# A fused two-layer transformer block on one core: operand rows moved 32 bytes apart, and one layer's products in another order

## The chip, the cores and the metric

The kernel runs on one core of one Trainium2 chip. The metric is the device time of the whole program in microseconds; lower is better.

## What is computed

Two layers work on 512 tokens of width 1024, all in float32. Layer 1 is differential attention with a feed-forward block, layer 2 is sliding-window attention with sinks and a feed-forward block. Cut to what matters here:

```python
def swiglu(h, w_gate_up, w_down):
    g, u = jnp.split(h @ w_gate_up, 2, axis=-1)
    return (jax.nn.silu(g) * u) @ w_down

def reference(x, ...):
    for l in range(DEPTH):                       # DEPTH = 2
        h = rms_norm(x, attn_norm[l])
        x = x + (diff_attention(h, ...) if l == 0 else swa_sink_attention(h, ...))
        x = x + swiglu(rms_norm(x, ffn_norm[l]), w_gate_up[l], w_down[l])
    return x
```

The gate and up weights have 2816 columns each, and the kernel takes them in 11 column blocks of 256.

## The kernel before

**Three matmuls for one.** Every operand of a large product is kept as a high part and a low part, both in TensorE's rounded float32 type. ScalarE rounds a value into the high part (`hi`) and VectorE writes the rest into the low part (`lo`). One product is then three matmuls: high by high, high by low, low by high. This makes TensorE, ScalarE and VectorE all busy.

**Buffers.** Weight parts lie in two rings of eight buffers each, `hi` and `lo`, of 512 words per partition (four rows of 128, two of 256, or one of 512). They are made in `parts` (attention and the first column block) and in `Ffn.split` (the rest). The input of a layer, normed and turned so that tokens run along the free axis, is `hTh` and `hTl`: eight rows `k` of 512 tokens (`new_hT`). In `Ffn.rest` the kernel also makes `th` and `tl`, three sums and differences of quarters of the turned input, four rows of 256 tokens each.

**Starts of operands.** SBUF addresses below are bytes in a partition. Before the change `hTh` starts at 28672, `hTl` at 45056, the `lo` ring at 61440, the `hi` ring at 86016, all multiples of 256, and every row in them is 512, 1024 or 2048 bytes long. So every row starts at 0 mod 256. `th` and `tl` start at 128 mod 256, with rows of 1024 bytes.

**Feed-forward.** Column block 0 is multiplied in `start`, block 1 in `up`. Blocks 2 to 10 of each layer go through `up7`, which forms the four quarter products of a 2 x 2 split with seven products instead of eight (Strassen's way, in Winograd's form). There are two sides `c` (gate and up), so fourteen products a block, each with four rows `k` and three matmuls a row, 256 columns wide: 12 matmuls. The order of the products of a block is fixed by a list at the end of `up7`; `block(n)` says what the moving operand is. In this order two products read the turned input (24 matmuls), four read the sums (48), six read the turned input (72), and the last two read the sums (24). The stationary operand is the weight part, the moving one the input. The down products (`down`) follow in groups: blocks 0 and 1, then 2 to 4, 5 to 7, 8 to 10. They are 512 wide, stationary `ah` or `al` and moving `hi` or `lo`; their matmul is at line 809.

**What sets the order.** TensorE's order is the order of the program text. `Flow` lets the preparation of weight parts run up to six products ahead of TensorE (`AHEAD`), with the rings' eight buffers as limit. The low part of products 1 and 5 of a list (`DLO`) is made by a transfer that adds into `lo` instead of by VectorE.

**Other matmuls on these buffers.** `mm3` (lines 292 to 294) holds three matmuls for attention's projections (512 or 256 wide; there the turned input is stationary and the weight part moves), for the output projections (stationary `oh`, `ol`, moving weight parts) and for column blocks 0 and 1.

The lines of the profile that matter: L721 is the matmul in `up7`, L809 the one in `down`, L292 to L294 the three of `mm3`, L585 and L587 the making of `hi` and `lo`.

Of the kernel before, what the change touches and what calls it, by code (L numbers as in the profile page):

```python
# [9 lines left out]
F32 = mybir.dt.float32  # L10
F32R = mybir.dt.float32r
# [6 lines left out]
P = 128  # L18
S = 512
NT = S // P  # L20
D = 1024
KT = D // P
# [15 lines left out]
NTH = 3  # L38
# [3 lines left out]
EVAC = 6  # L42
RAWB = 2
HLB = 8
TDB = 2
QB = 4
AFTER_A = 2
# [90 lines left out]
def tile_yoco_hybrid(  # L138
# [95 lines left out]
    def rsq(dst, v, n):  # L234
# [8 lines left out]
        for it in range(3):  # L243
# [4 lines left out]
                eng.scalar_tensor_tensor(w, w, -0.5, v, op0=ALU.mult, op1=ALU.mult)  # L248
            eng.scalar_tensor_tensor(dst if it == 2 else y, w, 1.5, y, op0=ALU.add, op1=ALU.mult)

    class Split:


# [8 lines left out]
    def parts(unit, raw, h, gains=None, by_cols=False):  # L262
        a, b = raw.shape[1:]
        part = raw[:, :, h * b // 2:(h + 1) * b // 2] if by_cols else raw[:, h * a // 2:(h + 1) * a // 2, :]
        hi = wp.tile(list(part.shape), F32R, name=nm("hi"), tag="hi", bufs=HLB)
        lo = wp.tile(list(part.shape), F32R, name=nm("lo"), tag="lo", bufs=HLB)
        if gains is None:
            nc.scalar.copy(hi, part)  # L268
            nc.vector.tensor_tensor(lo, part, hi.bitcast(F32), op=ALU.subtract)  # L269
        else:  # L270
            w = b // len(gains)
            for i in range(a // 2):
                for n, gs in enumerate(gains):
                    g, cs = gs[h * a // 2 + i], slice(n * w, (n + 1) * w)
                    nc.scalar.activation(hi[:, i, cs], part[:, i, cs], AF.Copy, scale=g)
                    nc.vector.scalar_tensor_tensor(lo[:, i, cs], part[:, i, cs], g, hi[:, i, cs].bitcast(F32),
                                                   op0=ALU.mult, op1=ALU.subtract)
        unit.halves.append((hi, lo))
# [20 lines left out]
            nc.vector.tensor_tensor(lo, src, hi.bitcast(F32), op=ALU.subtract)  # L299

    def new_hT():
        hh = xp.tile([P, KT, S], F32R, name=nm("hTh"), tag="hTh", bufs=1)
        hl = xp.tile([P, KT, S], F32R, name=nm("hTl"), tag="hTl", bufs=1)
        return hh, hl

    def transpose_in(hT, src, t, h):
        pt = att()
# [195 lines left out]
    class Ffn:  # L503
        def __init__(self, layer, np_):
            self.np = np_
            self.wu = w_gate_up[layer].rearrange("(k p) n -> p k n", p=P)
            self.wd = w_down[layer].rearrange("(k p) n -> p k n", p=P)
            self.xn = {}
            self.hT = None
            self.gb = []  # L510
            for h in range(2):
                gb = np_.tile([P, 512], F32, name=nm("gb"), tag="t", bufs=4)
                nc.gpsimd.dma_start(out=gb, in_=ffn_norm[layer, h * 512:(h + 1) * 512].partition_broadcast(P))
                self.gb.append(gb)
# [62 lines left out]
                    queue.dma_start(out=r[:, c], in_=self.wu[:, 4 * j:4 * j + 4, c * FFN + q * 256:c * FFN + (q + 1) * 256])  # L577

        def split(self, src, shape, move=False):
            hi = wp.tile(shape, F32R, name=nm("hi"), tag="hi", bufs=HLB)  # L580
            lo = wp.tile(shape, F32R, name=nm("lo"), tag="lo", bufs=HLB)
            if move:
                nc.scalar.activation(lo, src, AF.Copy, scale=-1.0)  # L583
                nc.gpsimd.dma_start(out=lo.bitcast(F32), in_=src, accum_op=ALU.add)  # L584
            nc.scalar.copy(hi, src)  # L585
            if not move:
                nc.vector.tensor_tensor(lo, src, hi.bitcast(F32), op=ALU.subtract)  # L587
            return hi, lo
# [88 lines left out]
        def up7(self, flow, q):  # L677
# [34 lines left out]
            def product(f, c, b, n, fresh):  # L712
                def go():
                    if fresh:
                        bank[b, c] = acc() if b == "X" else att("po") if (b, c) == ("Z", 1) else att()
                    hi, lo = parts[f, c]
                    bh, bl = self.block(n)
                    dst = bank[b, c][:, 0:256]
                    for k in range(4):
                        for i, (l, r) in enumerate(((hi, bh), (hi, bl), (lo, bh))):  # L720
                            nc.tensor.matmul(dst, l[:, k, :], r[:, k, :], start=fresh and k == 0 and i == 0,  # L721
                                             stop=k == 3 and i == 2, skip_group_check=not fresh)
                    if (f, c) == ("11", 0):
                        self.new_lf(q)
                        self.uc = self.fp.tile([P, 3, 256], F32, name=nm("uc"), tag="uc", bufs=1)
# [135 lines left out]
        def rest(self, fp, hook, done, out=False):  # L861
            self.fp = fp
            self.lf, self.gs, self.rs, self.ready = {}, {}, {}, {0: -1}
            self.th, self.tl = (fp.tile([P, n + NTH * 1024], F32R, name=nm(z), tag=z)[:, m:m + NTH * 1024]
                                .rearrange("p (n k q) -> p n k q", k=4, q=256)
                                for z, n, m in (("th", 416, 416), ("tl", 96, 0)))
            for z in ("ah", "al"):
                fp.tile([P, 256], F32R, name=nm(z), tag=z, bufs=AHB)
            for q, j in ((1, 0), (1, 1), (2, 0)):
                self.load_r(q, j, FIRST(nc))  # L870
            if FAST:
                for _ in self.tokens():
                    pass
            flow = Flow({"w": HLB, "a": AHB})
            flow.step(lambda: self.first_pair())
            self.ready[0] = 0
            chunks = [(0, 1), (2, 3, 4), (5, 6, 7), (8, 9, 10)]
            for qs in chunks:
                for q in qs:
                    if q:  # L880
                        (self.up7 if q in FAST else self.up)(flow, q)
                        if q == 1 and NTH == 3 and 1 not in FAST:
                            flow.step(lambda: self.later())
                end = qs is chunks[-1]
                self.down(flow, qs, end and ("out" if out else "mid"), hook if end else {}, done)
            flow.run()
# [264 lines left out]
            return (DA_STEPS3 if self.p == 3 else DA_STEPS)(T, C, U, W, N, B)  # L1151

    with tc.tile_pool(name="da", bufs=1, reuse_waits="tile") as ap:
        ap.tile([P, 96], F32, name="pad")
        Cd = ap.tile([P, NT, 2, P], F32, name="Cd")
        Sd = ap.tile([P, NT, 2, P], F32, name="Sd")
        pairs = [Pair(ap, p) for p in range(4)]
# [96 lines left out]


    with tc.tile_pool(name="ffn0", bufs=1, reuse_waits="tile") as fp:
        fp.tile([P, 96], F32, name="pad")
        nxt = {}

        def lead(t):  # L1260
            def go():
                if not nxt:
                    nxt[0] = new_hT()
                transpose_in(nxt[0], xs[:, t, :], t, 0)
            return go

        ffn.rest(fp, {6: {(0, 0): lead(2), (0, 2): lead(3), (1, 0): lead(0), (1, 1): lead(1)}}, lambda t, ns: None)
# [2 lines left out]


    with tc.tile_pool(name="sw", bufs=1, reuse_waits="tile") as ap:
        ap.tile([P, 96], F32, name="pad")
        gq = [gT[:, 8 + k:9 + k] for k in range(KT)]
        gkv = [gT[:, 16 + k:17 + k] for k in range(KT)]
        Cs = ap.tile([P, NT, 2, HD], F32, name="Cs")
# [229 lines left out]
        ffn.start({1: lambda: ffn.turn(2), 3: lambda: ffn.turn(3)})  # L1506

    with tc.tile_pool(name="ffn1", bufs=1, reuse_waits="tile") as fp:
        fp.tile([P, 96], F32, name="pad")
        ov = out[0].rearrange("(t p) d -> p t d", p=P)  # L1510
        ffn.rest(fp, {}, lambda t, ns: nc.sync.dma_start(out=ov[:, t, ns], in_=xs[:, t, ns]), True)

# [33 lines left out]
```

## Time and profile before

| | before |
|---|---|
| median of 3 runs | 1123.99 us (1123.21 to 1125.3) |
| span of the profiled execution | 1121.8 us, 2.2 us under that median |
| TensorE matmul, weight load | 1101.6 us (98%), 978.3 us (87%) |
| VectorE, ScalarE | 1008.4 us (90%), 711.3 us (63%) |
| granted TensorE clock | 1.000 over the whole span |
| up products at L721 | first at 335.9 us, last at 1089 us |

The profiled execution's own time outside its span is not recorded; only the span is. In the rows of groups, the first number is busy time, the second the mean duration of one in ns, then the engine's idle time just before. Durations of matmuls overlap, since the next one starts before the last column of the one before has left the array; the distance from start to start is read from the timeline, whose first column is the start in us.

### The profile page before, as it was taken

What the parts mean: (1) busy time and instruction counts of PE and PEld (TensorE: products, weight loads), DVE (VectorE), ACT (ScalarE), POOL (GpSimd) and SP (SyncE); (2) the same over time, 40 slices, a digit from 0 to 9 for tenths busy, and PEclk for the clock granted to TensorE, in tenths of its full rate; (3) what the DMA queues carried; (4) which work ended last, traced back from release to release, by engine and by line L of the source; (5) the groups of instructions that cost most, each with busy time, mean ns of one, the idle gap of its engine ahead of it and who ended that gap; (6) DMA issues with size and microseconds to landing.
All of it is one profiled execution on the core that took longest, in us unless ns stands there. A gap on an engine that the chain in (4) does not pass through costs nothing.

```text
span 1121.8 us, 20162 instructions
## 1 busy us (share of the span) xinstructions
PE 1101.6 (98%) x7206; PEld 978.3 (87%) x7206; DVE 1008.4 (90%) x2418; ACT 711.3 (63%) x1577; POOL 55.5 (5%) x76
## 2 busy tenths in 40 slices
PE   8999999999999999999999999999999999999998
PEld 6878888778989989989998778878989989998997
DVE  5979798979999899999998787988899999899997
ACT  6575756454555665675678499697555666566574
POOL 1100000000000010010003000000010000000000
PEclk9999999999999999999999999999999999999999
DMA  6312121124453434336124311120545247246213
GB/s 198 113 57 77 38 77 50 65 72 140 146 162 98 141 80 160 112 82 203 57 48 106 111 41 57 39 76 25 198 138 168 76 104 207 85 104 178 77 30 103
DMA packets 94085, 114.90 MB, mean 102 GB/s; under 512 B 5993, under 2 KB 70914, under 8 KB 93986
## 3 DMA queue, kind: packets, MB, share of 16 engines
q1 hardware_dynamic: 87216, 100.97, 28.1%
q0 software_dynamic: 6720, 12.65, 6.3%
q8 instruction: 56, 0.92, 0.3%
q14 instruction: 43, 0.35, 0.1%
q10 hardware_dynamic: 50, 0.01, 0.0%
HBM read 99.98 MB, written 2.10 MB: 91 GB/s over the span
## 4 chain that ended last, share of the span: by engine, by line
PE 77%; DVE 12%; ACT 6%; DMA 2%; issue 1%; SPq 1%; DVEq 0%; ACTq 0%
PE acc L721 16%; PE tr L721 10%; PE tr L809 9%; PE acc L809 8%; PE acc L292 8%; PE acc L294 8%; PE acc L293 8%; PE po L721 2%; PE tr L435 2%; ACT s L1399 2%; DVE hss L385 1%; ACT s L1406 1%; DVE lo L587 1%; DMA r<-in_w_gate_up_dram 1%; PE tr L310 1%
## 5 line engine op out<-in xcount | busy, mean ns | idle before, releaser
L585 ACT CAST hi<-r 128x512 fp32r<-128x512 f32 x160 | 98.9, 620 | 79.5 <-PE acc L721 35.8
L292 PE MATMUL acc<-hi,hTh 128*128 128x512 f32 (+1 forms) x352 | 132.9, 377 | 2.5 <-DVE vl L1022 1.4
L293 PE MATMUL acc<-lo,hTh 128*128 128x512 f32 (+1 forms) x352 | 124.1, 353 | 0.4 <-DVE lo L269 0.4
L294 PE MATMUL acc<-hi,hTl 128*128 128x512 f32 (+1 forms) x352 | 124.2, 353 | 0.1
L585 ACT CAST hi<-g 128x512 fp32r<-128x512 f32 x154 | 94.9, 618 | 40.8 <-PE acc L293 19.2
L587 DVE TENSOR_TENSOR lo<-r,hi 128x512 fp32r<-128x512 f32 x160 | 105.3, 692 | 6.1 <-ACT hi L585 5.8
L585 ACT CAST hi<-raw 128x512 fp32r<-128x512 f32 x108 | 66.9, 621 | 62.5 <-PE tr L721 18.2
L792 ACT CAST ah<-lf 128x256 fp32r<-128x256 f32 x154 | 61.1, 404 | 47.9 <-PE tr L809 16.0
L721 PE MATMUL acc<-hTh,lo 128*128 128x256 f32 x288 | 81.6, 283 | 0.0
L721 PE MATMUL acc<-hTl,hi 128*128 128x256 f32 x288 | 81.5, 283 | 0.0
L721 PE MATMUL acc<-hTh,hi 128*128 128x256 f32 x288 | 81.5, 283 | 0.0
L721 PE MATMUL acc<-tl,hi 128*128 128x256 f32 x288 | 81.2, 282 | 0.0
L721 PE MATMUL acc<-th,hi 128*128 128x256 f32 x288 | 81.1, 282 | 0.0
L721 PE MATMUL acc<-th,lo 128*128 128x256 f32 x288 | 81.1, 282 | 0.0
L268 ACT CAST hi<-raw 128x512 fp32r<-128x512 f32 x96 | 57.3, 619 | 33.9 <-PE acc L294 24.6
L292 PEld LDWEIGHTS acc<-hi,hTh 128*128 128x128 f32 x352 | 66.7, 190 | 13.4 <-issue 2.6
L587 DVE TENSOR_TENSOR lo<-g,hi 128x512 fp32r<-128x512 f32 x110 | 76.1, 692 | 1.5 <-ACT hi L585 1.4
L294 PEld LDWEIGHTS acc<-hi,hTl 128*128 128x128 f32 x352 | 66.5, 189 | 10.1 <-DVE hTl L907 0.7
L584 POOL DMA_DIRECT2D lo<-g x44 | 38.5, 976 | 716.4 <-ACT lo L583 372.3
L587 DVE TENSOR_TENSOR lo<-raw,hi 128x512 fp32r<-128x512 f32 x108 | 73.4, 692 | 0.0
L269 DVE TENSOR_TENSOR lo<-raw,hi 128x512 fp32r<-128x512 f32 x96 | 64.7, 688 | 9.4 <-ACT hi L268 8.9
L293 PEld LDWEIGHTS acc<-lo,hTh 128*128 128x128 f32 x352 | 66.9, 190 | 6.5 <-DVE lo L269 0.7
(280 smaller groups left out, 3644.7 us busy)
## 6 DMA issues: line engine op xcount, KB each, us to landing
r<-in_w_gate_up_dram SPq DMA_DIRECT2D x80, 512.0 KB, 5.0
g<-in_w_down_dram SPq DMA_DIRECT2D x88, 256.0 KB, 5.4
lo<-g POOLq DMA_DIRECT2D x44, 256.0 KB, 3.8
raw<-in_da_w_qkv_dram SPq DMA_DIRECT2D x30, 256.0 KB, 3.3
raw<-in_da_w_qkv_dram SPq DMA_DIRECT2D x8, 512.0 KB, 3.7
raw<-in_da_w_o_dram SPq DMA_DIRECT2D x8, 512.0 KB, 3.7
raw<-in_w_gate_up_dram SPq DMA_DIRECT2D x8, 512.0 KB, 3.7
raw<-in_sw_w_o_dram SPq DMA_DIRECT2D x8, 512.0 KB, 3.8
```

Of the source, the lines that this page charges most:

```text
L268: nc.scalar.copy(hi, part)
L269: nc.vector.tensor_tensor(lo, part, hi.bitcast(F32), op=ALU.subtract)
L292: nc.tensor.matmul(dst, sh, mh, start=start, stop=False)
L293: nc.tensor.matmul(dst, sh, ml, start=False, stop=False)
L294: nc.tensor.matmul(dst, sl, mh, start=False, stop=stop)
L435: nc.tensor.matmul(banks[c][:, cols], q[a][rows], k[b][rows], start=a + b == 0, stop=a == 1)
L584: nc.gpsimd.dma_start(out=lo.bitcast(F32), in_=src, accum_op=ALU.add)
L585: nc.scalar.copy(hi, src)
L587: nc.vector.tensor_tensor(lo, src, hi.bitcast(F32), op=ALU.subtract)
L721: nc.tensor.matmul(dst, l[:, k, :], r[:, k, :], start=fresh and k == 0 and i == 0, stop=k == 3 and i == 2, skip_group_check=not fresh)
L792: nc.scalar.copy(ah, src)
L809: nc.tensor.matmul(bank, l[:, tk], r, start=fresh and i == 0 and n == 0, stop=i == len(qs) - 1 and n == 2, skip_group_check=not fresh)
```

## The change

Buffers get 8 words (32 bytes, `SKEW`) of unused space. Each buffer of the `hi` and `lo` rings is 520 words long instead of 512, so the eight buffers start at 0, 32, ..., 224 mod 256. Each row of `hTh` and `hTl` is 520 words long, so row `k` starts at 32k mod 256. Each row of `th` and `tl` is 264 words long; `th` starts at 128 and `tl` at 0 mod 256, and every row starts 32 bytes further on. Padding in the pools keeps the other buffers on the places mod 256 that they had. The twelve matmuls of a product in `up7` are written in another order in layer 2 alone: four rows of high by high, then four of low weight by high input, then four of high weight by low input.

```diff
+SKEW = 8
...
+    def part_tiles(shape):
+        return [wp.tile([P, 512 + SKEW], F32R, name=nm(z), tag=z, bufs=HLB)[:, 0:512]
+                .rearrange("p (a b) -> p a b", b=shape[2]) for z in ("hi", "lo")]
...
-        hi = wp.tile(list(part.shape), F32R, name=nm("hi"), tag="hi", bufs=HLB)
-        lo = wp.tile(list(part.shape), F32R, name=nm("lo"), tag="lo", bufs=HLB)
+        hi, lo = part_tiles(part.shape)
...
-        hh = xp.tile([P, KT, S], F32R, name=nm("hTh"), tag="hTh", bufs=1)
-        hl = xp.tile([P, KT, S], F32R, name=nm("hTl"), tag="hTl", bufs=1)
-        return hh, hl
+        return [xp.tile([P, KT, S + SKEW], F32R, name=nm(z), tag=z, bufs=1)[:, :, 0:S] for z in ("hTh", "hTl")]
...
+            self.rows_first = layer == 1
...
-                    for k in range(4):
-                        for i, (l, r) in enumerate(((hi, bh), (hi, bl), (lo, bh))):
-                            nc.tensor.matmul(dst, l[:, k, :], r[:, k, :], start=fresh and k == 0 and i == 0,
-                                             stop=k == 3 and i == 2, skip_group_check=not fresh)
+                    terms = ((hi, bh), (hi, bl), (lo, bh))
+                    order = [(k, i) for i in (0, 2, 1) for k in range(4)] if self.rows_first else \
+                            [(k, i) for k in range(4) for i in range(3)]
+                    for k, i in order:
+                        l, r = terms[i]
+                        nc.tensor.matmul(dst, l[:, k, :], r[:, k, :], start=fresh and (k, i) == order[0],
+                                         stop=(k, i) == order[-1], skip_group_check=not fresh)
...
-            self.th, self.tl = (fp.tile([P, n + NTH * 1024], F32R, name=nm(z), tag=z)[:, m:m + NTH * 1024]
-                                .rearrange("p (n k q) -> p n k q", k=4, q=256)
-                                for z, n, m in (("th", 416, 416), ("tl", 96, 0)))
+            w = NTH * 4 * (256 + SKEW)
+            self.th, self.tl = (fp.tile([P, n + w], F32R, name=nm(z), tag=z)[:, m:m + w]
+                                .rearrange("p (n k q) -> p n k q", k=4, q=256 + SKEW)[:, :, :, 0:256]
+                                for z, n, m in (("th", 512 - 96, 512 - 96), ("tl", 96 - 64, 0)))
...
-        ap.tile([P, 96], F32, name="pad")
+        ap.tile([P, 352], F32, name="pad")
```

The order on TensorE differs in layer 2's `up7` only. Before, the first product of layer 2's block 2 stands as follows (moving operand first, then the stationary one):

```order
L721 MATMUL acc_10736<-hTh_9615,hi_10656 128x256
L721 MATMUL acc_10736<-hTl_9616,hi_10656 128x256
L721 MATMUL acc_10736<-hTh_9615,lo_10657 128x256
L721 MATMUL acc_10736<-hTh_9615,hi_10656 128x256
L721 MATMUL acc_10736<-hTl_9616,hi_10656 128x256
L721 MATMUL acc_10736<-hTh_9615,lo_10657 128x256
```

With the change, the same product and the one behind it, where `x4` stands for the four rows `k`:

```order
L726 MATMUL acc_10736<-hTh_9615,hi_10656 128x256 x4
L726 MATMUL acc_10736<-hTh_9615,lo_10657 128x256 x4
L726 MATMUL acc_10736<-hTl_9616,hi_10656 128x256 x4
L726 MATMUL acc_10756<-hTh_9615,hi_10670 128x256 x4
L726 MATMUL acc_10756<-hTh_9615,lo_10671 128x256 x4
L726 MATMUL acc_10756<-hTl_9616,hi_10670 128x256 x4
```

The first use of `lo` moved from the third matmul to the fifth, and its last use from the twelfth to the eighth. On VectorE, ScalarE, GpSimd and the transfer queue the order is the same; only shapes are written differently, as here for the sums on VectorE, before and after:

```order
L613 TENSOR_TENSOR tl_3734<-g_3746,th_3733 128x1024
```
```order
L615 TENSOR_TENSOR tl_3734<-g_3746,th_3733 128x4x256
```

More of the change, by code (lines that the diff above doesn't have):

```diff
@@ L579, in split @@
         def split(self, src, shape, move=False):
-            hi = wp.tile(shape, F32R, name=nm("hi"), tag="hi", bufs=HLB)
-            lo = wp.tile(shape, F32R, name=nm("lo"), tag="lo", bufs=HLB)
+            hi, lo = part_tiles(shape)
             if move:
@@ L1256, in tile_yoco_hybrid @@
     with tc.tile_pool(name="ffn0", bufs=1, reuse_waits="tile") as fp:
-        fp.tile([P, 96], F32, name="pad")
+        fp.tile([P, 352], F32, name="pad")
         nxt = {}
@@ L1272, in tile_yoco_hybrid @@
     with tc.tile_pool(name="sw", bufs=1, reuse_waits="tile") as ap:
-        ap.tile([P, 96], F32, name="pad")
+        ap.tile([P, 352], F32, name="pad")
         gq = [gT[:, 8 + k:9 + k] for k in range(KT)]
@@ L1508, in tile_yoco_hybrid @@
     with tc.tile_pool(name="ffn1", bufs=1, reuse_waits="tile") as fp:
-        fp.tile([P, 96], F32, name="pad")
+        fp.tile([P, 352], F32, name="pad")
         ov = out[0].rearrange("(t p) d -> p t d", p=P)
```

## Prediction

> **What bounds the kernel now.** I read the page first, for the engine that is never free, then the windows of the feed-forward stages, then TensorE's timeline row by row, because the change touches where TensorE's operands lie and nothing that an engine computes.
>
> ```profile
> span 1121.8 us, 20162 instructions
> PE 1101.6 (98%) x7206; PEld 978.3 (87%) x7206; DVE 1008.4 (90%) x2418; ACT 711.3 (63%) x1577; POOL 55.5 (5%) x76
> ...
> PEclk9999999999999999999999999999999999999999
> ...
> PE 77%; DVE 12%; ACT 6%; DMA 2%; issue 1%; SPq 1%; DVEq 0%; ACTq 0%
> PE acc L721 16%; PE tr L721 10%; PE tr L809 9%; PE acc L809 8%; PE acc L292 8%; PE acc L294 8%; PE acc L293 8%; PE po L721 2%; PE tr L435 2%; ACT s L1399 2%; DVE hss L385 1%; ACT s L1406 1%; DVE lo L587 1%; DMA r<-in_w_gate_up_dram 1%; PE tr L310 1%
> ```
>
> TensorE is busy 98% of the span, its clock is never throttled, and the chain that ended last is 77% TensorE. L721, the up products, is the largest part of that chain (16 + 10 + 2%). So time is matmuls multiplied by the distance from one start to the next. The windows show how much room the next engine leaves: first the up and the down products of layer 1's first full group of column blocks, then the sum over the six such groups of both layers.
>
> ```profile
> core 0: us, PE busy (x) PEld busy (x) DVE busy (x) ACT busy (x) POOL busy (x), PEclk, DMA share, GB/s
> 335.90:393.40 57.50, 57.50 (x483) 57.48 (x482) 54.00 (x95) 34.52 (x71) 1.72 (x2) 1.00 0.41 123
> 396.10:425.50 29.40, 28.63 (x127) 23.39 (x126) 29.40 (x59) 20.33 (x44) 3.53 (x4) 1.00 0.45 114
> ```
> ```profile
> sum 531.30, PE 529.73 PEld 499.23 DVE 503.71 ACT 334.79 POOL 32.55; mean PE 88.29 PEld 83.20 DVE 83.95 ACT 55.80 POOL 5.42
> ```
>
> In the up part (335.9 to 393.4 us) TensorE has no idle time and VectorE has 57.5 - 54.0 = 3.5 us of it; in the down part (396.1 to 425.5 us) VectorE is busy for all 29.4 us. A faster matmul is therefore worth its full price in the up part, and next to nothing in that down part. Over the six groups VectorE is idle 531.3 - 503.7 = 27.6 us: the feed-forward stages cannot gain more than that.
>
> **How far apart the matmuls are.** The timeline of TensorE, 256 columns wide: a run of 48 matmuls that read the sums (`th`, `tl`), then a run of 72 that read the turned input (`hTh`, `hTl`), then 512 columns wide: nine right after a stall, and nine long after one.
>
> ```profile
> 448.70 0.28 PE L721 MATMUL tr<-th,hi 128*128 128x256 f32 x1
> ...
> 454.40 0.28 PE L721 MATMUL tr<-hTh,hi 128*128 128x256 f32 x1
> ...
> 463.03 0.28 PE L721 MATMUL acc<-th,hi 128*128 128x256 f32 x1
> ```
> ```profile
> 101.32 0.40 PE L293 MATMUL acc<-lo,hTh 128*128 128x512 f32 x1
> ...
> 103.41 0.39 PE L293 MATMUL acc<-lo,hTh 128*128 128x512 f32 x1
> ```
> ```profile
> 316.88 0.39 PE L809 MATMUL tr<-hi,ah 128*128 128x512 f32 x1
> ...
> 318.92 0.39 PE L809 MATMUL po<-hi,ah 128*128 128x512 f32 x1
> ```
>
> (454.40 - 448.70)/48 = 118.8 ns for the sums; (463.03 - 454.40)/72 = 119.9 ns for the turned input. 512 wide it is (103.41 - 101.32)/9 = 232 ns after a stall, (318.92 - 316.88)/9 = 226.7 ns when settled. From 256 to 512 columns the settled distance grows by 106.8 ns, 0.417 ns a column; 256 columns at that rate are 107 ns, so 13 ns of each distance are not streaming. Two things say that part of these 13 ns depends on how the weight load's read meets the moving operand's. The one SBUF difference between the two 256-wide runs is the start: the turned input begins at 0 mod 256 bytes, like the weights, and the sums at 128. And the same 512-wide form at the same remainders takes 232 or 226.7 ns, by how the two streams stand to each other. The durations show the same:
>
> ```profile
> engine op xcount: duration ns min/median/max, first and last start us, forms
> L721 PEld LDWEIGHTS acc<-hTh,hi x288: 187/192/193, 335.7 to 1081.5; 128*128 128x128 f32 x144
> L721 PE MATMUL acc<-hTh,hi x288: 277/283/284, 335.9 to 1081.7; 128*128 128x256 f32 x144
> ...
> L721 PEld LDWEIGHTS acc<-th,hi x288: 187/188/193, 341.5 to 1088.7; 128*128 128x128 f32 x144
> L721 PE MATMUL acc<-th,hi x288: 279/281/286, 341.6 to 1088.8; 128*128 128x256 f32 x144
> ```
>
> With equal remainders the load sits at 192 ns, near its maximum, and the matmul at 283, near its maximum: a stable, rather bad meeting. At 128 the load is at 188, its best being 187, and matmuls spread from 279 to 286. No matmul of these groups is more than 6 ns better than the median (277 against 283), none more than 5 worse (286 against 281).
>
> **The change, part by part.** No matmul, copy or transfer is added or taken away. Counts of the matmuls besides L721 that meet the skewed buffers:
>
> ```profile
> L292 PE MATMUL acc<-hi,hTh 128*128 128x512 f32 x224 | 95.0, 424 | 2.5 <-DVE vl L1022 1.4 <-ACT hTh L906 1.1
> ...
> L292 PE MATMUL acc<-hi,oh 128*128 128x512 f32 x128 | 54.6, 426 | 0.0
> ...
> L292 PE MATMUL acc<-hi,hTh 128*128 128x256 f32 x128 | 37.8, 296 | 0.0
> L292 PE MATMUL acc<-hTh,hi 128*128 128x256 f32 x128 | 36.5, 285 | 0.0
> ...
> L292 PE MATMUL acc<-hTh,hi 128*128 128x512 f32 x64 | 24.9, 390 | 0.0
> ```
>
> - Layer 2's up products, 9 column blocks x 14 products x 12 = 1512 matmuls. Their moving rows now begin 32 bytes further on at every step and return to the first place after four (4 x 32 bytes), while the stationary rows keep one remainder; no two neighbours meet alike. The mean today is (4 x 119.9 + 3 x 118.8)/7 = 119.4 ns, since four of the seven kinds of product read `hT`. Ends: 6 ns less and 5 more. I take -2.5 ns, between the change seen from 0 to 128 (-1.1) and the best seen (-6), because here no position is held: -3.8 us.
> - Layer 1's up products on `hT`, 864: the order stays, so three neighbours share a row. I take what 128 against 0 shows, -1.1 ns: -1.0 us. The 648 on the sums already differ from their weights: 0, ends -2 and +5 ns.
> - The other 256-wide matmuls on `hT`, 2 groups x 3 lines x 128 = 768, at -1.1 ns: -0.8 us.
> - The 512-wide ones (3 x (224 + 128 + 64) = 1248, and the down products): they settle at 226.7 and stand at 232 when disturbed. Mixed remainders may keep them from settling. I take 0: in L292 to L294 many stand unsettled already, and in the first down part VectorE is the bound. Ends: below.
> - Rows that are no longer contiguous. `hT` and the sums are written and read in four pieces.
>
> ```profile
> L587 DVE TENSOR_TENSOR lo<-r,hi 128x512 fp32r<-128x512 f32 x160 | 105.3, 692 | 6.1 <-ACT hi L585 5.8
> ...
> L299 DVE TENSOR_TENSOR hTl<-tr,hTh 128x512 fp32r<-128x512 f32 x24 | 16.0, 686 | 4.3 <-ACT hTh L298 4.2
> ```
>
>   Four pieces of 128 took 686 ns where one of 512 took 692: 0. The 44 accumulating transfers into `lo` land 32 to 224 bytes past a 256-byte boundary. They are made six products (6 x 12 x 0.12 = 8.6 us) ahead of their use: 0 while that cover stands; without it, TensorE would wait for each.
> - Waits in layer 2. The first matmul that needs `lo` moves from the third to the fifth of a product (0.24 us later), the last from the twelfth to the eighth: VectorE's result is due later and its buffer free sooner. `hi` is held to the twelfth as before. TensorE has no wait in the up part to shorten: 0.
>
> Sum: -3.8 - 1.0 - 0.8 = -5.6 us. The profiled span of 1121.8 becomes 1116.2; the median of the runs shown is 2.2 us above that span, which I leave as it is: 1124.0 - 5.6 = 1118.4, in round numbers 1118.5 us.
>
> **Rivals.** *Nothing happens* (1124 us): the 1.1 ns between the runs come from something else than the start, and mixed remainders average out to what stands now. For it: only two remainders occur in this trace and they differ by 1%. Against it: within L721 the load's 192 against 188 ns goes with the start. [...]
>
> *Slower*, by one mechanism: the 512-wide matmuls lose their settled distance. At the unsettled 232 instead of 226.7 ns, the 924 down products cost 924 x 5.3 = 4.9 us, and some half of the 1248 others 3.3 us: 8.2 us, with the up products' gain at nothing 1124 + 8 = 1132, with half of it 1129. It decides from the point where the rise on these 1548 matmuls exceeds 5.6/1548 = 3.6 ns. For it: nine in a row at 232 ns with the very same operands. Against it: the unsettled ones appear only after stalls, and where VectorE is the bound a longer matmul hides.
>
> *Much faster*: every 256-wide matmul reaches its best. On `hT` these are 4/7 of 3024 = 1728 up products and the 768 others, 2496 x 6 ns = 15.0 us; on the sums 1296 x 2 ns = 2.6 us; together 17.6 us, which gives 1106 us. VectorE's 27.6 us would still allow it. Against it: the best distance is seen singly, never kept.
>
> **How the numbers follow.** The forecast and its neighbourhood have 0.50, much faster (below 1112) 0.10, nothing 0.21, slower 0.19. The measurement can tell about 0.2% (2.2 us) from no change; the first two are faster by more, so 0.60, 0.21 and 0.19. The range runs from 1106, the bound of much faster, to 1129, the slower rival with half the gain kept; beyond them I leave some 2 in 10. The likeliest case alone: 1112 to 1121.
>
> **What would show it.** In the timeline of after, 72-matmul runs on `hT` in layer 2 shorter than 8.63 us, by the forecast about 117 ns a matmul; in layer 1 about 119. Weight loads of `hT` products nearer 188 than 192 ns. Down products still at 227 ns in their last part, and VectorE's busy time as before. The prediction is wrong if the runs stay at 120 ns, if 512-wide matmuls stand at 230 ns or more throughout, or if VectorE's share shows it waiting for TensorE no longer while TensorE idles in the up parts.

## The result and the profile after

The kernel became slower by 0.2%: 1127.13 us (1125.91 to 1128.79, 12 runs) against 1124.45 us (1122.83 to 1128.2, 12 runs) for the kernel before on the same chip, ratio 1.002 with a 95% interval of 1.0011 to 1.003. Ratios here and below come from runs interleaved on one chip and differ a little from the quotient of the medians. The profiled span went from 1121.8 to 1124.0 us. Three lines of the page of after, the span, the engines and the shares of the chain that ended last:

```profile
span 1124.0 us, 20134 instructions
...
PE 1104.5 (98%) x7206; PEld 974.4 (87%) x7206; DVE 1010.6 (90%) x2418; ACT 712.6 (63%) x1577; POOL 55.4 (5%) x76
...
PE 82%; DVE 9%; ACT 5%; DMA 2%; issue 1%; SPq 0%; DVEq 0%; ACTq 0%
```

TensorE is still the bound and holds more of the chain (82 for 77%), VectorE less (9 for 12%). So the matmuls themselves moved. TensorE's timeline of after, first the up products in layer 1 (48 on the sums, then 72 on the turned input, to the next run on the sums), at the place shown of before:

```profile
449.06 0.28 PE L726 MATMUL tr<-th,hi 128*128 128x256 f32 x1
...
454.71 0.28 PE L726 MATMUL tr<-hTh,hi 128*128 128x256 f32 x1
...
463.23 0.28 PE L726 MATMUL acc<-th,hi 128*128 128x256 f32 x1
```

That is (454.71 - 449.06)/48 = 117.7 ns for 118.8 before, and (463.23 - 454.71)/72 = 118.3 ns for 119.9. In layer 2 the view merges the four rows of one kind:

```profile
1033.86 0.65 PE L726 MATMUL tr<-th,hi 128*128 128x256 f32 x4
...
1039.58 0.63 PE L726 MATMUL tr<-hTh,hi 128*128 128x256 f32 x4
...
1048.10 0.64 PE L726 MATMUL acc<-th,hi 128*128 128x256 f32 x4
```

119.2 ns on the sums and 118.3 ns on the turned input: a small gain again, and no more with the new order than without it. The 512-wide down products went the other way, early and late alike; nine distances each:

```profile
318.08 0.40 PE L814 MATMUL tr<-hi,ah 128*128 128x512 f32 x1
...
320.18 0.39 PE L814 MATMUL po<-hi,ah 128*128 128x512 f32 x1
```
```profile
1028.23 0.40 PE L814 MATMUL tr<-hi,ah 128*128 128x512 f32 x1
...
1030.33 0.40 PE L814 MATMUL tr<-hi,ah 128*128 128x512 f32 x1
```

Both are 2.10/9 = 233 ns where the settled ones of before had 226.7; the median of all 923 distances went from 227 to 231 ns. They do not settle any more. The 512-wide matmuls of the first column block show it in their mean duration, 393 to 395 ns in after's groups where before's had 389 to 390:

```profile
L296 PE MATMUL acc<-hTh,hi 128*128 128x512 f32 x64 | 25.3, 395 | 0.0
```

Adding up the distances from each start to the next over whole kinds of matmuls gives the account:

| us, by summed distances | before | after | |
|---|---|---|---|
| up products on the turned input, layer 1 (864) | 103.55 | 102.15 | -1.40 |
| the same, layer 2 (864) | 103.55 | 102.52 | -1.03 |
| up products on the sums, layer 1 (648) | 76.99 | 76.64 | -0.35 |
| the same, layer 2 (648) | 76.99 | 76.99 | 0 |
| down products (923 distances) | 212.29 | 214.96 | +2.67 |
| column block 0, 512 wide on the turned input (192) | 43.58 | 44.60 | +1.02 |
| 512-wide moving weights, attention and output (1056) | 266.77 | 267.75 | +0.98 |
| 256 wide on the turned input in blocks 0 and 1 (384) | 46.65 | 47.11 | +0.46 |
| all, first to last matmul | 1115.76 | 1117.99 | +2.23 |

The up products gave 2.8 us, the 512-wide matmuls took 4.7.

### The profile page after: what moved, and what is told of

It reads as the page before. It is cut to its first block, busy times and chain, and to the rows that moved or that the text cites. A ratio compares the mean times of both kernels' runs of the same rounds, so it can differ in the third digit from the quotient of the medians.

```text
span 1124.0 us, 20134 instructions
## 1 busy us (share of the span) xinstructions
PE 1104.5 (98%) x7206; PEld 974.4 (87%) x7206; DVE 1010.6 (90%) x2418; ACT 712.6 (63%) x1577; POOL 55.4 (5%) x76
## 4 chain that ended last, share of the span: by engine, by line
PE 82%; DVE 9%; ACT 5%; DMA 2%; issue 1%; SPq 0%; DVEq 0%; ACTq 0%
PE acc L726 18%; PE tr L726 11%; PE tr L814 9%; PE acc L296 8%; PE acc L814 8%; PE acc L298 8%; PE acc L297 8%; PE po L726 2%; PE tr L437 2%; ACT s L1405 2%; DVE lo L273 1%; ACT s L1412 1%; DVE hss L387 1%; PE po L814 1%; PE tr L312 1%; PE po L297 1%
## 5 line engine op out<-in xcount | busy, mean ns | idle before, releaser
L726 PE MATMUL acc<-hTh,hi 128*128 128x256 f32 x288 | 63.5, 281 | 0.0
L726 PE MATMUL acc<-th,hi 128*128 128x256 f32 x288 | 63.5, 281 | 0.0
L726 PE MATMUL acc<-tl,hi 128*128 128x256 f32 x288 | 63.4, 281 | 0.0
L726 PE MATMUL acc<-th,lo 128*128 128x256 f32 x288 | 63.4, 281 | 0.0
L726 PE MATMUL acc<-hTh,lo 128*128 128x256 f32 x288 | 63.3, 281 | 0.0
L726 PE MATMUL acc<-hTl,hi 128*128 128x256 f32 x288 | 63.3, 281 | 0.0
```

## The experiments

Theory A: TensorE falls into a settled rhythm when neighbouring matmuls begin alike, and mixing the starts breaks it. Theory B: each pair of starts has a price of its own, whatever its neighbours are. Both are put against a rival, theory C in the expectations: the time went elsewhere (waits, the new order, the rows in pieces). "Settled" means that the distances from start to start repeat in a short cycle; a settled distance is the mean of that cycle.

**Each start by itself (`starts`).** A kernel of matmuls alone, without the transformer: 48 times the same pair of operands, for moving operands that begin at 0, 32, ..., 224 mod 256 (`ma` to `mh`) with the weights at 0 (`sa`), then the weights at eight starts, then the two orders of a product.

```diff
+    for w in (256, 512):
+        for m in moving:                       # starts 0, 32, ..., 224
+            segment([(still[0], m[:, 0:w])] * 48)
+    for s in still:
+        segment([(s, moving[0])] * 48)
```

> The kernel leaves the whole block out and runs only matmuls: 48 in a row from one weight buffer and one moving buffer, for moving starts at 0, 32, ..., 224 mod 256 (ma to mh) with the weights at 0, 256 and then 512 columns wide; then the moving start at 0 and the weights at 0 to 224 (sa to sh), 512 wide; then two products of a column block on rows 32 bytes apart, in the old and in the new order, four times each. Theory A (a matmul that stands to the next weight load as its predecessor did settles; changing neighbours keep it unsettled, whatever the start): 256 wide 120 ns at 0 and 118.7 at 128, 512 wide 226.7 ns at 0 and at most other starts, the rows in both orders about 118.3 ns. Theory B (each start has its own price): 512 wide 226.7 ns only at 0, and 231 to 233 ns at 32 to 224, 256 wide 118 to 119 ns everywhere but at 0. Theory C (the longer matmuls of the changed kernel come from other engines): 120 and 226.7 ns in all segments.

TensorE's timeline of that kernel; the second column is the time that the 48 took:

```profile
24.53 6.01 PE L44 MATMUL acc<-ma,sa 128*128 128x256 f32 x48 [0.52 <-DVE xs L45]
...
37.44 5.71 PE L44 MATMUL acc<-mc,sa 128*128 128x256 f32 x48 [0.52 <-DVE xs L45]
43.67 6.01 PE L44 MATMUL acc<-md,sa 128*128 128x256 f32 x48 [0.52 <-DVE xs L45]
50.20 5.97 PE L44 MATMUL acc<-me,sa 128*128 128x256 f32 x48 [0.52 <-DVE xs L45]
...
63.10 5.71 PE L44 MATMUL acc<-mg,sa 128*128 128x256 f32 x48 [0.52 <-DVE xs L45]
...
75.79 11.21 PE L44 MATMUL acc<-ma,sa 128*128 128x512 f32 x48 [0.52 <-DVE xs L45]
87.79 11.46 PE L44 MATMUL acc<-mb,sa 128*128 128x512 f32 x48 [0.79 <-DVE xs L45]
100.03 11.28 PE L44 MATMUL acc<-mc,sa 128*128 128x512 f32 x48 [0.78 <-DVE xs L45]
```

The settled distances in these runs, from the single starts:

| moving start mod 256 | 0 | 32 | 64 | 96 | 128 | 160 | 192 | 224 |
|---|---|---|---|---|---|---|---|---|
| 256 wide, ns | 120.0 | 116.7 | 113.3 | 120.0 | 118.8 | 117.5 | 113.3 | 118.3 |
| 512 wide, ns | 226.7 | 233.3 | 228.9 | 233.3 | 232.1 | 234.2 | 233.3 | 233.3 |

The start sets the distance, and with the weights moved instead of the moving operand the 512-wide row came out mirrored (226.7, 233.3, 233.3, 234.3, 232.1, 233.3, 228.9, 233.3): what counts is the difference of the two. 0 and 128 reproduce the kernel before (119.9 and 118.8). Theory C is out for these distances: no other engine works while the 48 run (VectorE's 21.2 us of the 291.0 lie ahead of the segments and between them). B is nearly right for 512 columns: 226.7 ns belongs to start 0 alone, and my expectation under A, that most starts would settle there, was wrong. B's 118 to 119 ns for all other starts at 256 columns was wrong too. And B's prices do not add up in after. Sorted by the difference of the two starts in the built program, its up products take 118.1 to 118.7 ns on average at all eight differences, where this table goes from 113.3 to 120.0; its down products have medians of 230 to 233 ns, 231 at difference 0. With mixed neighbours nothing settles, as A says.

The two orders of one product on rows 32 bytes apart, at the end of this kernel, came out at 117.0 ns a matmul in the old order (46 distances from 271.06 to 276.44 us) and 118.5 in the new one (40 from 277.81 to 282.55 us). I had expected 118.3 for both: with spread rows the new order is the dearer one.

**The change in its halves (`rows_only`, `ring_only`, `old_order`).** One kernel spreads only the rows of the turned input and the sums, one only the rings, both with the old order; the third has the whole change but the old order in layer 2.

```diff
# rows_only, against after
-        return [wp.tile([P, 512 + SKEW], F32R, ...)[:, 0:512]
+        return [wp.tile([P, 512], F32R, ...)[:, 0:512]
...
# ring_only, against after: hTh, hTl
-xp.tile([P, KT, S + SKEW], F32R, ...)[:, :, 0:S]
+xp.tile([P, KT, S], F32R, ...)[:, :, 0:S]
# ring_only, against after: th, tl
-            w = NTH * 4 * (256 + SKEW)
+            w = NTH * 4 * 256
...
# all three
-            self.rows_first = layer == 1
+            self.rows_first = False
```

> Only the rows of the turned input and of the sums are 32 bytes apart; the weight rings start at 0 mod 256 as before, and the order is the old one. Theory A: down products (weights and left sides all at 0) are back at 227 ns, 2.7 us less than with the whole change; up products stay near 118.3 ns, so about 3.5 us less than before there; the first column block, 512 wide on the turned input, stays at 232 ns. Together 1122 to 1123 us against 1124.5 before, ratio 0.998 to 0.999. Theory B: down products at 227 ns too, but up products by their mean price; about the same time. Theory C: non-contiguous rows cost VectorE and ScalarE, so the time stays at 1126 us or more.

> Only the weight rings are 32 bytes apart; turned input and sums as before, old order. Theory A: down products at 231 to 233 ns as with the whole change, up products near 118.5 ns since neighbouring weight loads still differ between the high and the low buffer, attention's projections at 233 ns: 1126 to 1127 us, ratio 1.001 to 1.003. Theory B: the same. Theory C (rows): 1124.5 us as before, since no row is split.

> The whole change but the old order in layer 2 too. In the changed kernel layer 2's up products stand at 118.7 ns on average, layer 1's at 118.25. Theory A (the order matters as far as it changes how neighbours meet): layer 2 falls to 118.25 ns, 0.7 us less than the changed kernel, about 1126.4 us. Rival: the row order is what makes layer 2's products faster at all, as I forecast (2.5 ns each): they rise to above 119 ns and the time to 1128 us or more.

Sums of distances, spans and ratios to before, with the kernels of the next paragraphs:

| | up, us | down, us | block 0, 512 wide | span | ratio (95%) |
|---|---|---|---|---|---|
| before | 361.1 | 212.3 | 43.6 | 1121.8 | |
| after | 358.3 | 215.0 | 44.6 | 1124.0 | 1.002 (1.0011 to 1.003) |
| rows_only | 356.8 | 212.6 | 44.6 | 1119.3 | 0.9981 (0.9971 to 0.9992) |
| ring_only | 357.8 | 215.4 | 44.6 | 1124.6 | 1.0029 (1.0017 to 1.004) |
| old_order | 357.9 | 214.9 | 44.6 | 1125.9 | 1.0031 (1.0019 to 1.0044) |
| order_alone | 361.1 | 210.8 | 43.6 | 1121.1 | 0.9996 (0.9987 to 1.0006) |
| place_64 | 356.2 | 211.8 | 44.0 | 1118.2 | 0.9979 (0.9971 to 0.9988) |
| place_192 | 356.2 | 213.7 | 44.8 | 1118.6 | 0.9978 (0.9968 to 0.9987) |
| place_96 | 362.9 | 211.0 | 44.8 | 1125.6 | 1.0041 (1.0026 to 1.0056) |
| kick_32 | 356.2 | 210.6 | 44.0 | 1117.9 | 0.9976 (0.9964 to 0.9987) |
| kick_0 | 342.7 | 222.4 | 44.0 | 1117.4 | 0.9963 (0.9949 to 0.9977) |
| kick_0_less_dve | 342.7 | 227.6 | 44.0 | 1128.0 | 1.0024 (1.0007 to 1.004) |

The spans are of one profiled execution each, the ratios of all executions. The profiled executions of `old_order`, `kick_32`, `kick_0` and `kick_0_less_dve` have mean clocks of 0.998, 0.998, 0.997 and 0.992, which I put down to one, one, two and five stretches of 3.41 us at half the TensorE clock (last section), each worth some 1.7 us by my estimate (half of 3.41); the others have 1.000.

The change is a useful half and a harmful one. The down products' operands are all in the rings or in `ah` and `al`, which did not move; with the rings back at 0 their matmuls are back (first line, `rows_only`), with the skewed rings alone they are lost (second, `ring_only`). Durations, min/median/max, of the same group:

```profile
L814 PE MATMUL tr<-hi,ah x156: 387/389/468, 317.7 to 1094.2; 128*128 128x512 f32 x156
```
```profile
L814 PE MATMUL tr<-hi,ah x156: 387/393/468, 319.0 to 1099.0; 128*128 128x512 f32 x156
```

389 ns is what before has, 393 what after has. The up products gain in either half (4.3 and 3.3 us) and not twice in both together (3.2 in `old_order`), so the halves' ratios do not add up; in all three there are unlike neighbours, and why the rows alone do best was not tried by itself. `old_order` stays slower than before, so the new order is not the cause; its interval overlaps that of after, and its up products take 0.4 us less.

**The order alone, and three fixed places (`order_alone`, `place_64`, `place_192`, `place_96`).** The first is before with layer 2's products row by row. The others are before with every row of the turned input and the sums at one place, the rings at 0: 64 and 192 were best in `starts` at 256 columns, 96 as bad as 0.

```diff
# place_64: 16, place_192: 48, place_96: 24
+PLACE = 16
...
+        return [xp.tile([P, 64 + KT * S], F32R, name=nm(z), tag=z, bufs=1)[:, PLACE:PLACE + KT * S]
+                .rearrange("p (k s) -> p k s", s=S) for z in ("hTh", "hTl")]
...
-                                for z, n, m in (("th", 416, 416), ("tl", 96, 0)))
+                                for z, n, m in (("th", 384 + PLACE, 384 + PLACE), ("tl", 64 - PLACE, 0)))
...
# order_alone, against before: the loop of L721 as in after, rings and rows as in before
+            self.rows_first = layer == 1
```

> The kernel before with nothing but layer 2's products row by row. Theory A: every neighbour has the same remainder in either order, so the distances stay at 119.9 and 118.8 ns: 1124 us, ratio within 0.001 of 1. Rival (the order has a price of its own, by the later use of the low weight part or by the changed neighbours): 0.5 ns more on 1512 matmuls, 0.8 us, or a visible gain.

> As the run with 192, but all rows of the turned input and of the sums at 64 mod 256. Theory A: the same 113.3 ns in the up products; the first column block's 512-wide matmuls at 229 ns (0.4 us more than before) and the projections, 512 wide with the turned input as weights, at 233 ns once settled (2.7 us more). So 1 to 3 us more than the run with 192, that is 1105 to 1115 us. Rival: no difference from before, 1124 us.

> The kernel before, with one start for all rows of the turned input and of the sums: 192 mod 256 instead of 0 and 128; weights stay at 0, rows stay contiguous, old order. Theory A with the prices of the run on starts alone (one constant start settles on its own distance): up products 113.3 ns instead of 119.9 (1728 of them) and 118.8 (1296), which is 18.4 us less; the 768 other 256-wide ones on the turned input about 5 us less; the first column block's 512-wide ones 233 instead of 227 ns, 1.2 us more; down products at 227 ns as before. 22 us less, 1102 us, if VectorE keeps up; with VectorE busy for the whole of most down parts I expect 1104 to 1112 us. Rival (only changing starts matter, a constant one merely shifts the settling): 120 ns as at 0, 1124 us.

> As the run with 192, but all rows at 96 mod 256, a control. Theory A: up products at 120 ns, no gain on the turned input and 1.5 us more on the sums; 512-wide ones on the turned input at 233 to 234 ns, 4.5 us more; 256-wide projections 1 us less. 1127 to 1131 us, ratio 1.003 to 1.006. Rival (any start but 0 is better than 0): faster than before.

With all rows at one place the order changes neither the up products (361.1 us in both) nor the time (ratio 0.9996). The control at 96 did what it should: the up products at 120.0 ns on average, slower by 0.41%. 64 and 192 are faster, but by a miss: the up products stand at 117.8 ns, not at 113.3. The same 72 products at 64, first and last:

```profile
453.39 0.28 PE L721 MATMUL tr<-hTh,hi 128*128 128x256 f32 x1
...
461.87 0.28 PE L721 MATMUL acc<-th,hi 128*128 128x256 f32 x1
```

(461.87 - 453.39)/72 = 117.8 ns, and the mean over all 3024 is 117.8 in both kernels. So one start has more than one settled distance, and something chooses.

**What chooses (`kicks`).** Matmuls alone: 24 of 512 columns at start 0, then one other instruction or none, then 60 of 256 columns at 64 (`mc`) or 192 (`mg`).

```diff
+    for start in (2, 6):
+        for kick in (None, "turn", (0, 128), (0, 256), (1, 256), (3, 256), (4, 256), (1, 512), (4, 512)):
+            kicked(start, kick)        # the pair is (moving operand, columns)
```

> Matmuls alone, the rest of the block is left out. In the run on starts alone, 60 matmuls of 256 columns with the moving start at 64 or 192 mod 256 stood at 113.3 ns, each row begun after a pause; in the block with all rows at 192 or 64 they stand at 117.8 ns, coming straight from settled 512-wide matmuls. Here 24 matmuls of 512 columns (start 0) run straight into 60 of 256 columns at 64 (mc) and at 192 (mg), nine times each: with nothing between, or with one other matmul between (a transpose, 128 or 256 columns at 0, 256 at 32, 96 or 128, 512 at 32 or 128). Theory A, extended (a start has more than one settled distance, and what ran just before picks it): 117.8 ns with nothing between, and 113.3 ns after at least one of the eight others. Rival (the block's 117.8 ns come from other engines or from the changing weight buffers): 113.3 ns in all eighteen.

The timeline; `ks` is the one matmul between:

```profile
30.30 7.23 PE L45 MATMUL acc<-mc,sa 128*128 128x256 f32 x60
...
68.15 0.28 PE L63 MATMUL ks<-ma,sa 128*128 128x256 f32 x1
68.27 6.96 PE L45 MATMUL acc<-mc,sa 128*128 128x256 f32 x60
...
80.53 0.28 PE L63 MATMUL ks<-mb,sa 128*128 128x256 f32 x1
80.65 7.23 PE L45 MATMUL acc<-mc,sa 128*128 128x256 f32 x60
...
219.74 0.28 PE L63 MATMUL ks<-me,sa 128*128 128x256 f32 x1
219.86 6.98 PE L45 MATMUL acc<-mg,sa 128*128 128x256 f32 x60
```

(7.23 - 0.28)/59 = 117.8 ns without anything between, (6.96 - 0.28)/59 = 113.2 ns after one 256-wide matmul at start 0, 117.8 again after one at 32. For 192 it is one at 128 that does it. The other sixteen of the eighteen cases took 7.23 to 7.31 us and settled at 117.8. One earlier matmul decides in which of two settled distances the next sixty stand: history counts, which B does not allow. Why it is this matmul and no other was not tried.

**The kick in the kernel (`kick_0`, `kick_32`).** `place_64` with one extra matmul ahead of each of the six groups of up products, into an accumulator that the next product overwrites; at start 0, and as a control at 32.

```diff
+                    if (f, c) == ("11", 0) and q in (2, 5, 8):
+                        flat = hi.rearrange("p k q -> p (k q)")
+                        nc.tensor.matmul(dst, hi[:, 0, :], flat[:, 0:256], start=True, stop=True)
# kick_32: flat[:, 8:264]
```

> All rows of the turned input and of the sums at 64 mod 256, and one matmul more in front of each group of three column blocks (six in the program): 256 columns, moving start at 0, into the bank that the first product then starts afresh. In the run with matmuls alone such a one, behind settled 512-wide ones, put the following 60 at 113.3 instead of 117.8 ns. Theory A extended: the 3024 up products stand at 113.3 ns, 13.5 us less on TensorE than in the run with 64 alone; a group then needs 504 x 0.1133 + 126 x 0.2267 = 85.7 us of TensorE, as much as VectorE's work in it (85 to 87 us in four groups, 80 in the last ones), so VectorE becomes the bound and half of it is left: 1110 to 1116 us. Rival (the block's changing buffers do not keep the better distance): 117.8 ns, 1121 us.

> The same extra matmuls, but with their moving start at 32 mod 256. In the run with matmuls alone this one led to 117.8 ns. Theory A extended: up products at 117.8 ns as without it, 1121 us. Rival (any matmul more, or the short wait that it makes, is what helps): the same gain as with the start at 0.

The distances went as expected: 113.3 ns in all 3024 up products of `kick_0`, 117.8 in `kick_32`. That is 13.5 us less than in `place_64`, yet the span fell by 0.8 us, and the intervals of the two kernels overlap. By the median this is the fastest kernel run, 0.37% below before. The down products took 10.6 of the 13.5 us, 222.4 us for 211.8. The windows of the second down part, of before and of `kick_0`:

```profile
485.90:514.50 28.60, 28.60 (x128) 23.69 (x127) 28.60 (x57) 19.42 (x41) 3.15 (x4) 1.00 0.48 128
```
```profile
core 0: us, PE busy (x) PEld busy (x) DVE busy (x) ACT busy (x) POOL busy (x), PEclk, DMA share, GB/s
485.70:515.90 30.20, 28.85 (x129) 23.55 (x128) 30.20 (x61) 20.77 (x45) 3.51 (x4) 1.00 0.45 118
...
395.80:428.40 32.60, 30.51 (x128) 24.73 (x127) 31.56 (x63) 21.52 (x46) 3.53 (x4) 0.95 0.41 105
994.90:1026.60 31.70, 29.14 (x128) 23.50 (x127) 31.70 (x64) 21.43 (x46) 3.49 (x4) 1.00 0.43 114
```

The columns are the time of the window, then for each engine its busy time and number of instructions, the granted clock, the DMA share and GB/s. In before 128 matmuls and 57 VectorE instructions share 28.6 us, and both engines are busy throughout. In `kick_0` it is 61 VectorE instructions and 30.2 us; in the first down part 63 and 32.6 us where before had 59 and 29.4. VectorE is busy all of it or nearly, and TensorE has 1.35 and 2.1 us of idle time. My reading, which no run shows by itself: VectorE instructions that had been done during the longer up part are still to come. Part of the first down part's 32.6 us is a stretch at half clock (granted clock 0.95). All six executions of `kick_0` lost clock, with means of 0.995 to 0.998, and the one that lost least has the shortest span, 1115.4 us. The waits of `kick_0` (sum, times, longest, in us):

```profile
PEld tr L812 <- ACT hi L585: 9.1, 4, 2.7
...
PE tr L812 <- DVE xs L824: 7.5, 4, 2.3
```

These overlap in part, so they are not added up. The page of before names 1.5 us for the same group of matmuls, and its VectorE share of the chain is 12%; here it is 17%:

```profile
PE 71%; DVE 17%; ACT 6%; DMA 3%; issue 2%; SPq 1%; DVEq 0%; ACTq 0%
```

**Less work for VectorE (`kick_0_less_dve`).** A third product of a list has its low part made by a transfer instead of by VectorE.

```diff
-DLO = (1, 5)
+DLO = (1, 3, 5)
```

> As the run with six extra matmuls starting at 0, and one more product in each down list has its low weight part made by ScalarE and an adding transfer instead of VectorE (22 more in the program, 66 instead of 44). If VectorE is what took back the up products' gain, 22 x 0.69 = 15 us less on it lets the down products come closer to 227 ns: of the 11.7 us by which they became longer, 3 to 7 us come back, 1113 to 1117 us. Rival (the waits in the down part come from ScalarE, which now gets 22 x 0.62 us more, or from transfers that arrive late): no gain, or slower than the run without it.

A miss: ratio 1.0024 (1.0007 to 1.004), slower than before. VectorE's busy time did fall (995.1 us for 1006.3), but the down products took 227.6 us:

```profile
487.10:521.60 34.50, 30.73 (x129) 24.62 (x128) 32.27 (x63) 23.20 (x49) 6.20 (x7) 0.95 0.53 132
```

VectorE is no longer busy throughout (32.27 of 34.5 us), GpSimd has seven instructions in this part for four, and TensorE stands in longer waits: 9.9 us in four waits for VectorE, the longest 3.2 us, where `kick_0` had 7.5 and 2.3. More clock was lost as well: three down parts of this execution have a mean granted clock of 0.95, one of `kick_0`. That is not the whole of it, since at the same mean clock of 0.997 two executions here take 1122.8 and 1122.9 us where two of `kick_0` take 1117.4 and 1119.0. So VectorE as the only limit of the down part is not shown; the order in which ScalarE, VectorE and the transfers make the parts may be as much of it. What exactly binds the down part when the up part shrinks stays open.

## Why the prediction was wrong

The forecast was 1118.5 us, faster, and the result is slower. In its own terms: the up products gave 2.8 us where 4.8 were forecast, the other 256-wide matmuls on the turned input cost 0.5 where 0.8 were to be gained, and the 512-wide ones cost 4.7 where nothing was taken. Point by point:

- *512-wide matmuls: 0.* This step failed, and it turns the sign. The down products, column block 0 and the projections together cost 4.7 us, at medians by group of 231 to 235 ns where 226 to 234 stood. I had the mechanism as the "slower" rival and priced it at 8.2 us, since I let every one lose 5.3 ns; in the runs the down products lost 2.9 on average, some of it inside waits that were there anyway. What misled me was the argument that unsettled distances appear only after stalls: in `starts` each 512-wide start but 0 stays at 228.9 ns or more over 48 matmuls. The rival's condition, a rise above 3.6 ns on 1548 matmuls, would have decided against a gain of 5.6 us; with the real gain of 2.8 us half of that was enough. `ring_only` and `rows_only` show that the rings' spread causes the loss of the down products; that of column block 0 appears in both halves.
- *Layer 2's up products: -3.8 us.* Mis-sized: -1.0 (118.65 ns on the turned input where I named 117, and 118.8 unchanged on the sums). I put the value between the best single meeting and the only other start seen. Unlike neighbours give neither: they average over unsettled ones. The new order, which I took to help, is rather a loss with spread rows (118.5 against 117.0 ns in `starts`, 0.4 us between `old_order` and after).
- *Layer 1's on the turned input: -1.0 us.* Right in sign and nearly in size, -1.4, but by luck: I took the settled distance of start 128, and the 118.2 ns are a mean over unsettled meetings. The sums, taken as 0, gave -0.35.
- *The other 256-wide matmuls on the turned input: -0.8 us.* Not seen in the summed distances: +0.46 for those in blocks 0 and 1, though their median distance went from 120 to 118 ns (in layer 1 they hold waits that grew), and the moving-weight ones went from 49.76 to 49.83 us.
- *Weight loads at 188 ns instead of 192.* Seen in every up product of after, as here, and not worth what I read into it:

```profile
L726 PEld LDWEIGHTS acc<-hTh,hi x288: 187/188/193, 337.3 to 1082.5; 128*128 128x128 f32 x144
L726 PE MATMUL acc<-hTh,hi x288: 275/281/292, 337.5 to 1082.7; 128*128 128x256 f32 x144
```

  The matmuls' durations now spread over 17 ns (7 before): the spread of an unsettled stream, which the row shows at a glance.
- *Waits, rows in pieces, late transfers: 0.* Nothing speaks against it: `order_alone` is the same as before, `rows_only` with its rows in pieces is faster, and VectorE's busy time rose by 2.2 of 1008.4 us.
- *Rival "nothing happens".* The runs do not show the place to be free. In `starts` the settled distances are 113.3 to 120.0 ns at 256 columns and 226.7 to 234.2 at 512, by the start alone, with no other engine at work.
- *Rival "much faster".* The claim that the best distance is never kept was wrong: one distance of 113.3 ns was kept by 3024 matmuls in `kick_0`. The bound of 27.6 us that I took from VectorE's idle time was too generous: a gain of 18.4 us in the up products against before was worth 4.4 us of span. My reading is that the idle time in the up parts cannot be used for the work of the down parts; two stretches at half clock, by estimate some 3.4 us, took part of it too.

## What to carry to other kernels

A start of an operand is a tuning choice, and it belongs to a width: here 0 for 512 columns (226.7 ns, the others 228.9 to 234.2), 64 or 192 for 256 (113.3 ns, the others 116.7 to 120.0), relative to the weights. Give all neighbouring matmuls of a stage the same one: spread over a ring, the starts here cost the down products, which had the best, their settled distance (a median of 231 ns for 227). Measure it in a kernel of matmuls alone, but be ready for the stage to stand in another of its settled distances, as it did here (117.8 ns for 113.3), and look in the windows at what the second-busiest engine leaves before counting a gain.

## What the runs showed of the hardware that was not expected

One start and one form of matmul had two settled distances, 113.3 and 117.8 ns at 64 and at 192 of 256 in `kicks`. In the block at 64, one earlier matmul chose for the 504 of a group of column blocks that follow: 113.3 ns in `kick_0`, 117.8 in `kick_32`.

And TensorE's granted clock went to 0.50 after one wait of some 2 us and not after another. In `kick_0` the matmul at 406.27 us had waited 2.09 us for VectorE; the one at 1006.10 us 2.29 us:

```profile
406.27 0.47 PE L812 MATMUL tr<-hi,ah 128*128 128x512 f32 x1 [2.09 <-DVE xs L824]
...
408.23 0.63 PE L812 MATMUL tr<-hi,ah 128*128 128x512 f32 x1
408.66 0.63 PE L812 MATMUL tr<-lo,ah 128*128 128x512 f32 x1
```
```profile
1006.10 0.47 PE L812 MATMUL tr<-hi,ah 128*128 128x512 f32 x1 [2.29 <-DVE xs L824]
```
```profile
407.20:410.60 3.40, 3.40 (x10) 2.61 (x9) 3.40 (x8) 1.02 (x2) 0.00 (x0) 0.50 0.00 0
1003.00:1010.00 7.00, 4.71 (x21) 3.62 (x20) 7.00 (x15) 4.00 (x9) 0.00 (x0) 1.00 0.00 0
```
```profile
403.75:407.16 3.41, 1.32 (x6) 0.79 (x6) 3.41 (x7) 1.57 (x4) 0.00 (x0) 1.00 0.00 0
1001.08:1004.49 3.41, 2.73 (x13) 1.92 (x11) 3.41 (x8) 3.41 (x9) 0.00 (x0) 1.00 0.00 0
1004.49:1007.90 3.41, 1.80 (x8) 1.52 (x9) 3.41 (x7) 1.02 (x4) 0.00 (x0) 1.00 0.00 0
```

After the first, the granted clock (third column from the end) was 0.50 for 3.4 us and matmuls came 0.43 us apart; after the second it stayed at 1.00. By its mean clock of 0.997, `kick_0` has another such stretch, outside the six groups of column blocks; `old_order` and `kick_32` (0.998) have one and `kick_0_less_dve` (0.992) five, as I estimate from 1.7 us a stretch, and the profiled executions of before and after none while matmuls run. Other executions of before and after are likely to have had one, since some show a mean clock of 0.998, as the profiled one of `old_order` does.

The last three lines show what the two places differ in. In the trace of before the clock stays at full for 1116.16 us, in that of after for 1119.57 us. They differ by 3.41 us, the length of the stretch above, and are 327 and 328 times 3.413 us. Divided into windows of this length from where the clock fell, the first wait lies inside one window, in which TensorE was busy for 1.32 of 3.41 us (39%); the second is split between two, with 2.73 and 1.80 us busy (80 and 53%). Divided in the same way from where the clock rose, 5.10 and 4.83 us into the span, the lowest window up to the last matmuls is the one from 46.06 us in before (1.99 us busy, 58%) and from 45.79 us in after (2.16 us, 63%), and the clock stayed at full behind both; the window with the end of before's last matmul has 0.11 us busy (3%), and the clock fell at its end:

```profile
46.06:49.47 3.41, 1.99 (x12) 1.64 (x12) 3.41 (x8) 2.70 (x7) 0.00 (x0) 1.00 0.35 105
1117.85:1121.26 3.41, 0.11 (x1) 0.00 (x0) 0.75 (x2) 0.00 (x0) 0.00 (x0) 1.00 0.32 114
1121.30:1121.70 0.40, 0.00 (x0) 0.00 (x0) 0.00 (x0) 0.00 (x0) 0.00 (x0) 0.50 0.00 0
```

My reading from these windows, which no run tried by itself, is that the busy share of one window counted and not the length of the wait. By it, since the windows do not begin at the same time in every span, the same wait can fall inside one window in one execution and across two in the next.

So 2.09 us was enough in one place, and 2.29 us was not in another, and the first wait cost more than itself: some 1.7 us more by my estimate, half of 3.41, in which the clock was 0.50.
